# Rotating images by 180 degrees: whole 64 KB rows, three rotating slots, three transfers each way

## Chip, cores, metric

One core of a Trainium2 chip. The metric is the device time in microseconds; lower is better. The experiments ran on two chips (5, 6, 10 and 11 on one, the rest on the other), four to six executions each, always beside the kernel before, whose median was 123.67 to 123.75 us there.

## The reference

```python
def setup_inputs():
    batch, c, h, w = 32, 3, 256, 256
    return {"x": np.random.randn(batch, c, h, w).astype(np.float32)}

def reference(x):
    return np.rot90(x, k=2, axes=(-2, -1)).astype(np.float32)
```

There are 96 images of 256 KB. Rotating by 180 degrees reverses the 65,536 elements of each image. Nothing is computed: 25.17 MB come in, are reversed, and go out.

## The kernel before

Each image is cut into eight blocks of 32 KB. A pass takes 32 images: the first four blocks of each in `tinF`, the last four in `tinB`. Reversing the order of the blocks is left to the transfers' access patterns; reversing inside a block is done by VectorE, by copies of 128x4096 elements with a negative step. Each copy writes its own 16 KB tile, of which four rotate, and each tile is stored at once.

```python
# ... NG = 32 images, S = 8 blocks, BLK = 8192 elements, HB = 4096, Q = 4
tin_pool  = ctx.enter_context(tc.tile_pool(name="tin",  bufs=2))
tout_pool = ctx.enter_context(tc.tile_pool(name="tout", bufs=4))
for pp in range(n_pass):                      # 3 passes
    # ...
    nc.sync.dma_start(out=tinF[:, :], in_=x3[nsl, 0:Q, :])
    nc.sync.dma_start(out=tinB[:, :], in_=x3[nsl, S - 1:Q - 1:-1, :])

    tF0 = tout_pool.tile([P, HB], x.dtype, tag="t")
    nc.vector.tensor_copy(out=tF0[:, :], in_=tinB[:, 2 * HB - 1:HB - 1:-1])
    nc.scalar.dma_start(out=o4[nsl, 0:Q, 0, :], in_=tF0[:, :])
    # ... three more copies like this (tB0, tF1, tB1), each with its store
```

Of the kernel before, what the change touches and what calls it, by code (L numbers as in the profile page):

```python
# [2 lines left out]

os.environ.setdefault("NEURON_RT_ULTRASERVER_MODE", "4")

# [4 lines left out]


@with_exitstack
def kernel(
    ctx: ExitStack,
    tc: tile.TileContext,
    x: bass.AP,
    out: bass.AP,
):
    nc = tc.nc  # L20
    P = 128

    B, C, H, W = x.shape
    N = B * C
    L = H * W

    NG = 32
    Q = P // NG
    S = 2 * Q
    BLK = L // S  # L30

    HB = BLK // 2

    x3 = x.rearrange("b c h w -> (b c) (h w)").rearrange(
        "n (s e) -> n s e", s=S)
    o4 = out.rearrange("b c h w -> (b c) (h w)").rearrange(
        "n (s j f) -> n s j f", s=S, f=HB)

    tin_pool = ctx.enter_context(tc.tile_pool(name="tin", bufs=2))
    tout_pool = ctx.enter_context(tc.tile_pool(name="tout", bufs=4))  # L40

    n_pass = N // NG

    for pp in range(n_pass):
        nsl = slice(pp * NG, (pp + 1) * NG)
        tinF = tin_pool.tile([P, BLK], x.dtype, tag="F")
        tinB = tin_pool.tile([P, BLK], x.dtype, tag="B")
        nc.sync.dma_start(out=tinF[:, :], in_=x3[nsl, 0:Q, :])  # L48
        nc.sync.dma_start(out=tinB[:, :], in_=x3[nsl, S - 1:Q - 1:-1, :])

        tF0 = tout_pool.tile([P, HB], x.dtype, tag="t")
        nc.vector.tensor_copy(out=tF0[:, :], in_=tinB[:, 2 * HB - 1:HB - 1:-1])  # L52
        nc.scalar.dma_start(out=o4[nsl, 0:Q, 0, :], in_=tF0[:, :])

        tB0 = tout_pool.tile([P, HB], x.dtype, tag="t")
        nc.vector.tensor_copy(out=tB0[:, :], in_=tinF[:, 2 * HB - 1:HB - 1:-1])  # L56
        nc.scalar.dma_start(out=o4[nsl, S - 1:Q - 1:-1, 0, :], in_=tB0[:, :])

        tF1 = tout_pool.tile([P, HB], x.dtype, tag="t")
        nc.vector.tensor_copy(out=tF1[:, :], in_=tinB[:, HB - 1::-1])  # L60
        nc.scalar.dma_start(out=o4[nsl, 0:Q, 1, :], in_=tF1[:, :])

        tB1 = tout_pool.tile([P, HB], x.dtype, tag="t")
        nc.vector.tensor_copy(out=tB1[:, :], in_=tinF[:, HB - 1::-1])  # L64
        nc.scalar.dma_start(out=o4[nsl, S - 1:Q - 1:-1, 1, :], in_=tB1[:, :])


# [1 line left out]
_INS = ['x']  # L69
_OUTS = [((32, 3, 256, 256), 'float32')]  # L70


# [23 lines left out]
```

## Time and profile before

| | before |
|---|---|
| time, median | 123.75 us (123.7 to 123.9) |
| span of the profiled execution | 122.3 us |
| loads | 6 of 4 MB, rows of 32 KB, SyncE's queue (q1) |
| stores | 12 of 2 MB, rows of 16 KB, ScalarE's queue (q10) |
| VectorE | 12 copies, 27.2 us, 22% of the span |

Some words used below: a *packet* is what one transfer engine moves for a queue at one time, one row of a transfer here; a few bytes that only raise a semaphore are a packet too. A transfer is *issued* by an instruction of its queue's engine, and it has *landed* when its semaphore reports that all its data is there.

One view: that of who waited for whom. Its columns are total wait, number of waits, and the longest, in us.

```profile
DVE tF L52 <- DMA tinB<-in_x_dram: 41.2, 2, 23.4
DVE tF L60 <- DMA out_dram<-tF: 14.7, 2, 12.2
DVE tB L56 <- DMA out_dram<-tB: 11.1, 2, 8.4
```

VectorE stands still for up to 12 us until a store has left its tile. That costs nothing: the transfer engines have other tiles and loads in their queues all the while, and are busy for 99.6% of the time from 2.1 to 121.1 us.

### The profile page before, as it was taken

The numbers are of one execution on the slowest core, as the hardware profiler recorded it, in microseconds if no ns is written. First come the engines' busy times: TensorE is split into PE (matmuls) and PEld (weight loads), VectorE is DVE, ScalarE is ACT, GpSimd is POOL, SyncE is SP. The second block draws the span as 40 slices with busy tenths as digits, with TensorE's granted clock in tenths as the row PEclk, the third lists the DMA queues.
The fourth block names the chain that finished last, engine by engine and source line by source line (L and its number), as shares of the span: only waits on it lengthen the run. The fifth ranks groups of instructions, "written<-read, shape, count | busy, mean of one in ns | idle before, by whom it ended". The sixth has DMA issues, their size and how long they took to land.

```text
span 122.3 us, 93 instructions
## 1 busy us (share of the span) xinstructions
DVE 27.2 (22%) x12; POOL 0.2 (0%) x4
## 2 busy tenths in 40 slices
DVE  0000000399500000610160003307337156100000
POOL 0000000000000000000000000000000000000000
DMA  5798989899999998999999999999999999999992
GB/s 171 343 472 386 472 386 482 375 482 359 348 450 407 466 429 386 472 423 397 439 455 413 477 434 391 413 429 434 429 434 434 439 429 434 429 439 434 429 429 113
DMA packets 2592, 50.33 MB, mean 412 GB/s; under 512 B 288, under 2 KB 288, under 8 KB 288
## 3 DMA queue, kind: packets, MB, share of 16 engines
q1 hardware_dynamic: 864, 25.17, 48.9%
q10 hardware_dynamic: 1728, 25.17, 48.0%
HBM read 25.17 MB, written 25.17 MB: 412 GB/s over the span
## 4 chain that ended last, share of the span: by engine, by line
DMA 69%; DVE 11%; another core or an unknown queue 4%; SPq 0%; issue 0%; DVEq 0%
DMA out_dram<-tF 37%; DMA tinB<-in_x_dram 18%; DMA out_dram<-tB 14%; DVE tB L64 4%; DVE tF L60 4%; DVE tF L52 2%; DVE tB L56 2%; SPq L48 0%; DVEq L64 0%; DVEq L60 0%
## 5 line engine op out<-in xcount | busy, mean ns | idle before, releaser
L52 DVE COPY tF<-tinB 128x4096 f32<-128x4096 f32 x3 | 6.9, 2294 | 43.8 <-DMA tinB<-in_x_dram 41.2
L60 DVE COPY tF<-tinB 128x4096 f32<-128x4096 f32 x3 | 6.9, 2291 | 14.7 <-DMA out_dram<-tF 14.7
L56 DVE COPY tB<-tinF 128x4096 f32<-128x4096 f32 x3 | 6.9, 2292 | 11.1 <-DMA out_dram<-tB 11.1
L64 DVE COPY tB<-tinF 128x4096 f32<-128x4096 f32 x3 | 6.9, 2291 | 7.6 <-DMA out_dram<-tB 7.6
L80 POOL MEMSET const-bfloat16-1.0<- 128x1 bf16 x1 | 0.1, 102 | 0.0
L80 POOL MEMSET const-uint8-127<- 128x1 uint8 x1 | 0.1, 102 | 0.0
L80 POOL MEMSET const-float32-0.0<- 128x1 f32 x1 | 0.1, 99 | 0.2 <-issue 0.2
L80 POOL MEMSET const-float32-1.0<- 128x1 f32 x1 | 0.1, 99 | 0.0
## 6 DMA issues: line engine op xcount, KB each, us to landing
tinF<-in_x_dram SPq DMA_DIRECT2D x3, 4096.0 KB, 32.2
tinB<-in_x_dram SPq DMA_DIRECT2D x3, 4096.0 KB, 32.9
out_dram<-tF ACTq DMA_DIRECT2D x6, 2048.0 KB, 20.0
out_dram<-tB ACTq DMA_DIRECT2D x6, 2048.0 KB, 23.1
```

What stands on the lines that cost most here:

```text
L52: nc.vector.tensor_copy(out=tF0[:, :], in_=tinB[:, 2 * HB - 1:HB - 1:-1])
L56: nc.vector.tensor_copy(out=tB0[:, :], in_=tinF[:, 2 * HB - 1:HB - 1:-1])
L60: nc.vector.tensor_copy(out=tF1[:, :], in_=tinB[:, HB - 1::-1])
L64: nc.vector.tensor_copy(out=tB1[:, :], in_=tinF[:, HB - 1::-1])
L80: nc = _bacc.Bacc("TRN2", target_bir_lowering=False, num_devices=1)
```

## The change

The intent: fewer and larger transfers, with the longest row that stays contiguous in a partition, for the same 192 KB of each partition. An image becomes four rows of 64 KB. Three slots A, B and C of 64 KB rotate: load 0 into A, load 1 into B, turn A into C, load 2 into A, turn B into C, turn A into B. A turn is still four copies of 128x4096, but there is one store for all four. Turns 0, 1 and 2 below are these reversals; that two queues "take turns" on an engine is another matter.

```diff
-    tin_pool = ctx.enter_context(tc.tile_pool(name="tin", bufs=2))
-    tout_pool = ctx.enter_context(tc.tile_pool(name="tout", bufs=4))
+    pool = ctx.enter_context(tc.tile_pool(name="slots", bufs=1))
...  (S = 4 rows an image, E = 16384 elements, CH = 4 copies of F = 4096)
+    def load(g, slot):
+        t = pool.tile([P, E], x.dtype, tag=slot, name=f"in{g}")
+        nc.sync.dma_start(out=t[:, :], in_=x3[g * NG:(g + 1) * NG, :, :])
+        return t
+    def turn(g, t, slot):
+        r = pool.tile([P, E], x.dtype, tag=slot, name=f"out{g}")
+        for c in range(CH):
+            lo, hi = E - (c + 1) * F, E - c * F
+            src = t[:, hi - 1::-1] if lo == 0 else t[:, hi - 1:lo - 1:-1]
+            nc.vector.tensor_copy(out=r[:, c * F:(c + 1) * F], in_=src)
+        nc.scalar.dma_start(out=o3[g * NG:(g + 1) * NG, ::-1, :], in_=r[:, :])
...  (the loop over passes with its four copies and four stores goes)
+    a = load(0, "A")
+    b = load(1, "B")
+    turn(0, a, "C")
+    a = load(2, "A")
+    turn(1, b, "C")
+    turn(2, a, "B")
```

More of the change, by code (lines that the diff above doesn't have):

```diff
@@ L25 @@
     L = H * W
-    NG = 32
-    Q = P // NG
-    S = 2 * Q
-    BLK = L // S
-    HB = BLK // 2
+    S = 4
+    NG = P // S
+    E = L // S
+    CH = 4
+    F = E // CH
     x3 = x.rearrange("b c h w -> (b c) (h w)").rearrange(
         "n (s e) -> n s e", s=S)
-    o4 = out.rearrange("b c h w -> (b c) (h w)").rearrange(
-        "n (s j f) -> n s j f", s=S, f=HB)
-    tin_pool = ctx.enter_context(tc.tile_pool(name="tin", bufs=2))
-    tout_pool = ctx.enter_context(tc.tile_pool(name="tout", bufs=4))
@@ L42 @@
-    n_pass = N // NG
-    for pp in range(n_pass):
-        nsl = slice(pp * NG, (pp + 1) * NG)
-        tinF = tin_pool.tile([P, BLK], x.dtype, tag="F")
-        tinB = tin_pool.tile([P, BLK], x.dtype, tag="B")
-        nc.sync.dma_start(out=tinF[:, :], in_=x3[nsl, 0:Q, :])
-        nc.sync.dma_start(out=tinB[:, :], in_=x3[nsl, S - 1:Q - 1:-1, :])
-        tF0 = tout_pool.tile([P, HB], x.dtype, tag="t")
-        nc.vector.tensor_copy(out=tF0[:, :], in_=tinB[:, 2 * HB - 1:HB - 1:-1])
-        nc.scalar.dma_start(out=o4[nsl, 0:Q, 0, :], in_=tF0[:, :])
-        tB0 = tout_pool.tile([P, HB], x.dtype, tag="t")
-        nc.vector.tensor_copy(out=tB0[:, :], in_=tinF[:, 2 * HB - 1:HB - 1:-1])
-        nc.scalar.dma_start(out=o4[nsl, S - 1:Q - 1:-1, 0, :], in_=tB0[:, :])
-        tF1 = tout_pool.tile([P, HB], x.dtype, tag="t")
-        nc.vector.tensor_copy(out=tF1[:, :], in_=tinB[:, HB - 1::-1])
-        nc.scalar.dma_start(out=o4[nsl, 0:Q, 1, :], in_=tF1[:, :])
-        tB1 = tout_pool.tile([P, HB], x.dtype, tag="t")
-        nc.vector.tensor_copy(out=tB1[:, :], in_=tinF[:, HB - 1::-1])
-        nc.scalar.dma_start(out=o4[nsl, S - 1:Q - 1:-1, 1, :], in_=tB1[:, :])
+    o3 = out.rearrange("b c h w -> (b c) (h w)").rearrange(
+        "n (s e) -> n s e", s=S)
```

## The prediction

> **What bounds the kernel now.** I read four views: the slices and queues of the page, the queue tables of two stretches, and the engine in order of time. First the page, which says that nothing but the transfer engines can be the bound.
>
> ```profile
> span 122.3 us, 93 instructions
> ...
> DVE 27.2 (22%) x12; POOL 0.2 (0%) x4
> ...
> DMA  5798989899999998999999999999999999999992
> ...
> q1 hardware_dynamic: 864, 25.17, 48.9%
> q10 hardware_dynamic: 1728, 25.17, 48.0%
> ```
>
> VectorE works 22% of the span. The DMA row is full in every slice but the first few and the last. The queue of the loads (q1) and that of the stores (q10) fill 48.9 + 48.0 = 96.9% of 16 engines' span; asked for the stretch from 2.1 to 121.1 us, the same table gives 50.2 + 49.4 = 99.6%. So there is no hole in the middle, VectorE's waits on the stores cost nothing, and what lies outside is a start of 2.1 us and an end of 1.2 us.
>
> Second, how fast the engines work when only one direction runs (stores alone, 80 to 105 us), and third how the two directions share (30 to 45 us).
>
> ```profile
> DMA packets 738, 10.78 MB, mean 431 GB/s; under 512 B 80, under 2 KB 80, under 8 KB 80
> ...
> q10 hardware_dynamic: 738, 10.78, 100.7%
> ```
>
> ```profile
> q1 hardware_dynamic: 142, 4.13, 67.3%
> q10 hardware_dynamic: 135, 2.03, 31.6%
> ```
>
> In the first, 738 - 80 = 658 data packets of 16 KB take 100.7% of 16 x 25 us: 0.612 us each. From 5 to 20 us, loads alone, 203 packets of 32 KB fill 102.7% of 16 x 15 us: 1.214 us each. The durations of single packets in the trace are steadier still, 0.611 and 1.213. Twice 0.611 is 1.222, so a packet carries some 10 ns of its own and the rest is bytes. In the second fence the packets of both queues are nearly equal in number, 142 to 135, and the bytes go 2 to 1 with the packet sizes: an engine takes turns, one packet each. That is the fact on which the change depends.
>
> Fourth, when a store gets going behind a backlog of loads. The engine view in order of time:
>
> ```profile
> 23.36 2.29 DVE L52 COPY tF<-tinB 128x4096 f32<-128x4096 f32 x1 [23.36 <-DMA tinB<-in_x_dram]
> 25.56 2.29 DVE L56 COPY tB<-tinF 128x4096 f32<-128x4096 f32 x1
> 25.68 0.62 ACTq L53 DMA_DIRECT2D out_dram<-tF  x1
> 27.77 2.29 DVE L60 COPY tF<-tinB 128x4096 f32<-128x4096 f32 x1
> 27.88 0.55 ACTq L57 DMA_DIRECT2D out_dram<-tB  x1
> 29.97 2.29 DVE L64 COPY tB<-tinF 128x4096 f32<-128x4096 f32 x1
> 30.08 0.55 ACTq L61 DMA_DIRECT2D out_dram<-tF  x1
> 32.28 0.54 SPq L48 DMA_DIRECT2D tinF<-in_x_dram  x1
> ```
>
> The first store is issued at 25.68, but the queue table of 25.7 to 29.8 us holds packets of q1 alone; the first of q10 starts at 29.8, and the last engine gets to it at about 31.8. An issue on idle engines takes 1.4 us (first load issued at 0.73, first packet at 2.13); here it is 4.1 to 6.1 us: two or three load packets of 1.21 us that stand ahead are done first. Meanwhile four copies take 3 x 2.20 + 2.29 = 8.9 us.
>
> **What the Trainium skill says.** "DMA: Bandwidth & Descriptors", section "Queues, rings and completion order": each DMA engine goes round its queues at packet granularity. The 142 to 135 packets agree. The same section says that the semaphore's increment comes after the data of that engine; the 288 packets under 512 B (18 DMAs on 16 engines) are these, and in the trace such a packet also takes a turn in its queue. Section "Where 436 GB/s comes from" of that page gives a ceiling of 435.2 GB/s; the trace has 431 in the store-only stretch, so no change of shape can win much. "VectorE: DVE Perf Modes", "The perf-mode tier table", gives an fp32 SBUF copy of 2048 elements 1227 ns; the trace has 2294 ns for 4096, less than double, and the changed kernel keeps that same 128x4096 reversed copy.
>
> **The change, part by part.** Bytes are the same, 25.17 MB each way, and so are the twelve copies. SBUF stays at 192 KB a partition. 18 transfers become 6 of 8.39 MB; the packets should grow to 64 KB if a row goes as one packet. The copies no longer write four rotating 16 KB tiles, each stored as soon as it is turned, but one 64 KB slot that is stored when all four are done; and the second and third turns have no slot of their own: turn 1 writes C, which store 0 must leave first; turn 2 writes B, which turn 1 must have read.
>
> Gain. A 64 KB packet would be 4 x 0.602 + 0.010 = 2.417 us (0.602 is the difference of the two packet times above). Per engine 48 packets: 116.0 us. Before: 48 x 1.213 + 96 x 0.611 = 116.9 us, and 18 small ones. So 0.9 to 1.0 us is saved.
>
> Loss, followed in time on one engine. (1) Load 0 lands at 23.3 as the first 8.39 MB do now. Copies to 32.2; store 0 and load 2 are issued at 32.25 (now, too, the last of the first group's four stores goes at 32.29). (2) Load packet k ends at about 3.1 + 2.417 k (the slow first packets cost 0.6 in the trace). The store's first packet comes 4.1 to 6.1 us after issue, at 36.4 to 38.4, rounded up to the end of a 64 KB packet: packet 14 ends at 36.9, packet 15 at 39.35. I take 15. (3) Store 0 and the loads then take turns one to one: 8 store packets and 7 loads, 15 x 2.417 = 36.3, plus 0.7 for the stretched packets seen where the first store mixes in: the eighth ends at 76.3. By then 15 + 7 = 22 of 24 load packets are done; all loads are through at 76.3 + 2 x 2.417 = 81.1. (4) The semaphore packet waits for one more load packet, and the landing follows some 0.5 us after it, as for the first store now: 76.3 + 2.4 + 0.5 = 79.2. (5) Only now may turn 1 start in C: 8.9 us, store 1 is issued at 88.1, first packet 1.4 later at 89.5. From 81.1 to 89.5 the transfer engines have nothing: 8.4 us. (6) Turn 2 runs from 88.1 to 97 behind store 1, hidden; store 2 queues up behind it. 16 packets x 2.417 = 38.7, plus 1.0 for staggered and slow starts, plus the end of 1.2: span 89.5 + 40.9 = 130.4. The timed figure is 1.45 above the profile's span now (123.75 to 122.3): 131.9 us.
>
> With 14 load packets ahead the store ends one packet (2.4 us) earlier and three loads are left: 129.5. With 16 (three whole packets ahead of the store, as some engines had), 134.3. I put the middle at 131: the 15 case, leaning to 14 as 4.1 us alone would give it.
>
> **The rivals.** *Hidden anyway.* The loads that are left cover the 8.9 us of copies, and only the larger packets count: 123.75 - 1.0 = 122.8. For it speaks that VectorE waits up to 12 us for stores now at no cost. Against it: those waits are hidden by a backlog of other loads or of three other stored tiles, and here at most 2 or 3 load packets (5 to 7 us) are left against a semaphore, four copies and an issue, some 13 us. For the hole to close, store 0 would have to finish with six load packets left. *Short delay.* The store gets in 1.4 us after issue, behind the running packet only: 13 loads ahead, four left, hole near 3.6 us, time near 127.1. The 4.1 us of the trace speak against it, though that store was followed by three more issues, which may have held it up. *Rows cut smaller.* If rows go as 32 KB packets, the turns stay one to one: the store begins near 37, its 16 packets and 15 loads take 37.6 + 0.7, landing near 77.3, store 1 starts near 87.7, and the time is near 130: the same mechanism. Were loads cut and stores not, stores would get two thirds and the hole would vanish, 123; nothing speaks for that. *VectorE as the bound:* its total stays at 27 us, and no engine is near full. It matters only at the one place where its four copies stand alone.
>
> **Range and chances.** Predicted 131.0, 8 in 10 between 127.0 and 134.5: the low end is the short delay, the high end 16 packets ahead. Two per cent faster is 121.3, only 0.5 above 116.0 of packets, 2.1 of start, 1.2 of end and 1.45 outside the profile, with no slow packet and no hole at all, so 0.02. Within 2% needs the hole under 3.5 us: 0.08. Slower: 0.90.
>
> **What would show it.** In the changed profile: one hole in the DMA row, some 6 to 9 us, a little after two thirds of the span, with VectorE busy in it; the first copy of the second turn waiting for the first store, the longest wait after the start; six issues of 8192 KB; 64 KB packets, 384 a queue with 48 small ones each; store 0's landing 44 to 49 us after its issue; in the mixed stretch equal bytes on both queues. A full DMA row with about 122 us would prove the step from packets to turns wrong; a hole of another size, the count of load packets ahead of store 0; a stretch of lower GB/s, that large packets run at the same rate.

## More of the kernel before

Every execution was at a granted clock of 1.000, so only like is compared with like. The timed figure is some 1.8 us above the span of the same execution, which runs from its first to its last instruction.

## The result

The changed kernel takes 127.34 us (median of 4: 126.83, 126.83, 127.84, 128.04) against 123.8 us for the kernel before on the same chip. The ratio is 1.0293, 95% interval 1.0250 to 1.0337. Ratios here are the mean time of one kernel's fast runs over that of the other's of the same rounds, so not quite the ratio of the medians. The result is right on all outputs.

The page of the changed kernel (span, the DMA row of the 40 slices, the two queues):

```profile
span 125.0 us, 65 instructions
...
DMA  9779879977909779779977977709877977977790
...
q1 hardware_dynamic: 432, 25.17, 47.9%
q10 hardware_dynamic: 432, 25.17, 46.5%
```

Two things are to be seen. The queues hold 432 packets each, 384 of data and 48 small ones: a row of 64 KB is one packet. And their shares fell, from 96.9% to 94.4% of a longer span. The zeros in the DMA row need care: a slice is 3.1 us, a packet now 2.4 us, and the 16 engines run nearly in step, so a slice in which few packets start looks empty (the early zero near 35 us is such a one). Asking for single stretches settles it. The columns are the stretch and its length, VectorE's busy time, GpSimd's, the clock, the share of the transfer engines and GB/s:

```profile
2.10:81.00 78.90, 15.11 (x7) 0.00 (x0) 1.00 0.97 414
81.30:84.90 3.60, 3.57 (x3) 0.00 (x0) 1.00 0.00 0
84.90:124.00 39.10, 7.73 (x4) 0.00 (x0) 1.00 0.99 429
```

From 81.3 to 84.9 us no data moves at all, and VectorE is busy in 3.57 of the 3.60 us. From its last load packet to its first packet of store 1, an engine is idle for 3.9 us on the mean. Before and after it, the engines are as full as before the change. The chain of waits (start, duration, what) and VectorE's waits say what the hole is made of:

```profile
31.53 43.14 DMA out_dram<-out
74.66 0.03 issue
74.69 0.05 DVEq L56
74.74 0.05 issue
74.79 8.91 DVE out L56 x4
```

```profile
DVE out L56 <- DMA out_dram<-out: 43.3, 1, 43.3
```

Store 0 is issued at 31.53 and lands at 74.66. Only then may turn 1 write slot C. Its four copies take 8.91 us, to 83.70; store 1 is issued at 83.73, and its first packet starts at 84.95. The loads had their last packet through between 80.9 and 81.5. The wait that was 12 us long and free before is 43 us long, and the last 3.9 us of what follows it find the queues empty.

### The profile page after: what moved, and what is told of

It reads as the page before. It is cut to its first block, busy times and chain, and to the rows that moved or that the text cites. A ratio compares the mean times of both kernels' runs of the same rounds, so it can differ in the third digit from the quotient of the medians.

```text
span 125.0 us, 65 instructions
## 1 busy us (share of the span) xinstructions
DVE 26.7 (21%) x12; POOL 0.2 (0%) x4
## 3 DMA queue, kind: packets, MB, share of 16 engines
q1 hardware_dynamic: 432, 25.17, 47.9%
q10 hardware_dynamic: 432, 25.17, 46.5%
## 4 chain that ended last, share of the span: by engine, by line
DMA 52%; DVE 20%; DVEq 2%; issue 0%
DMA out_dram<-out 34%; DVE out L56 20%; DMA in<-in_x_dram 17%; DVEq L90 2%; DVEq L56 0%
## 5 line engine op out<-in xcount | busy, mean ns | idle before, releaser
L56 DVE COPY out<-in 128x4096 f32<-128x4096 f32 x12 | 26.7, 2289 | 65.9 <-DMA out_dram<-out 43.3
```

The lines of the kernel that those rows point to most:

```text
L56: nc.vector.tensor_copy(out=r[:, c * F:(c + 1) * F], in_=src)
```

## The experiments

All edits are against the changed kernel unless said otherwise. The theory under test, called "turns" below: the two queues take turns packet by packet; how many load packets are left when store 0 lands decides how much of the chain behind it (landing, four copies, issue) is covered. The rivals: packets of 64 KB cost time as such; the scheme of slots costs as such; VectorE, at 21% of the span, cannot matter.

### 1 and 2: is the bare chain on the path?

First, each copy of the second turn twice.

```diff
-            nc.vector.tensor_copy(out=r[:, c * F:(c + 1) * F], in_=src)
+            for _ in range(2 if g == 1 else 1):
+                nc.vector.tensor_copy(out=r[:, c * F:(c + 1) * F], in_=src)
```

> The changed kernel with each of the four copies of the second turn done twice. Theory: these copies lie on the path that ends the hole, so the hole grows from 3.8 to 12.7 us: 135.7 us, 8.9 more than the changed kernel's 126.8. Rival 'copies are hidden beside transfers' (VectorE is busy 21% of the span): no change, 127.

Measured: 136.06 us (135.55 to 136.78), ratio to the kernel before 1.0996. The profiled execution has a span of 133.8 us, 8.8 more than the changed kernel's, and in the view of single stretches the hole has grown to 81.3 to 93.7 us:

```profile
81.30:93.70 12.40, 12.37 (x7) 0.00 (x0) 1.00 0.00 0
```

Four copies more, 8.8 us more: these copies lie on the path in full.

Second, the same for the third turn (`g == 2`).

> The changed kernel with each of the four copies of the third turn done twice. Theory: they lie beside store 1, which runs to 104.4 us; the doubled turn ends near 101.4 and store 2 is issued before store 1 ends: no change, 126.8 to 128. A rival in which VectorE work as such costs time gives 135.7 here as for the second turn.

Measured: 127.32 us (126.58 to 127.87), ratio 1.0282, as the changed kernel. The same 8.8 us of VectorE work, put beside store 1, is free. So it is neither VectorE's load as such nor "copies are hidden": where they stand decides.

### 3 and 4: packet sizes, with a side effect

To shift the turns, one direction's rows are cut in two. First the loads:

```diff
-        nc.sync.dma_start(out=t[:, :], in_=x3[g * NG:(g + 1) * NG, :, :])
+        for h in (slice(0, E // 2), slice(E // 2, E)):
+            nc.sync.dma_start(out=t[:, h], in_=x3[g * NG:(g + 1) * NG, :, h])
```

> The changed kernel with each load as two transfers of 32 KB rows, stores and copies untouched (the half that the first copy needs is loaded last, so nothing starts earlier). Theory (turns): with 32 KB load packets against 64 KB store packets store 0 gets two thirds of the bandwidth, its eight packets end near 63 us instead of 71.4 to 73.9, it lands near 65, turn 1 is done near 74, and store 1 starts while loads are still queued: no hole (before the copies' end the DMA row is full), 123.0 us, a little faster than the kernel before. Rival 'large packets cost': loads at 32 KB give back at most half of the loss, 125 us or more, and the hole stays. Rival 'the slot scheme itself costs' (two turns that must wait for a slot): about 127, as the changed kernel.

Measured: 130.05 us (129.9 to 130.08), ratio 1.0507: a plain miss by 7 us. The trace shows the old hole gone (the queues move 421 GB/s from 60 to 80 us) and a new one from 101 to 107.4. The view of single stretches first, then the engines in order of time (start, duration, what, and in brackets the wait before it):

```profile
101.00:107.40 6.40, 4.49 (x2) 0.00 (x0) 1.00 0.07 31
```

```profile
77.08 4.49 DVE L57 COPY out<-in 128x4096 f32<-128x4096 f32 x2 [0.95 <-DMA in<-in_x_dram]
101.68 4.49 DVE L57 COPY out<-in 128x4096 f32<-128x4096 f32 x2 [20.10 <-DMA in<-in_x_dram]
```

The third turn's last two copies waited 20 us for one half of load 2, which landed at 101.7. On 14 of the 16 engines the loads' data was through by 84.1 us. Two had fallen behind between 45 and 67 us, where some of their 32 KB packets took up to 2.1 us instead of 1.21; store 1 then came between their last loads, turn by turn, to 98.9. So a late load packet is caught by the store's turns just as a late store is by the load's. Why two engines fell behind is open; all four runs have the time. The promise that nothing would start early was not kept either: the first two copies ran at 12.83 us, on the half that had landed. The built program has the copies of that half in front: the order of the source is not kept where the data allow another.

Then the stores:

```diff
-        nc.scalar.dma_start(out=o3[g * NG:(g + 1) * NG, ::-1, :], in_=r[:, :])
+        for h in (slice(E // 2, E), slice(0, E // 2)):
+            nc.scalar.dma_start(out=o3[g * NG:(g + 1) * NG, ::-1, h], in_=r[:, h])
```

> The changed kernel with each store as two transfers of 32 KB rows, both issued after all four copies; loads at 64 KB. Theory (turns): store 0 now gets one third while loads are queued, the ten load packets that are left are through near 75 us, store 0 ends last near 81, and the whole chain of landing, four copies and issue (0.8 + 8.9 + 1.3 = 11 us) lies bare: hole near 11 us, 134 us, 7 us slower than the changed kernel. Rival 'large packets cost': smaller store packets help, below 127.

Measured: 129.77 us (129.54 to 130.03), ratio 1.0484: slower, so the rival falls, but 4 us short of what was expected. Store 0 did land at 81.8, as expected. But the hole is 6.2 us, not 11: one half is issued after two copies, not four (at 27.19 in the first turn); the built program again has another order than the source. The two copies that are missing from the chain are 4.4 us.

### 5 and 6: packet sizes alone

Both experiments again, with one transfer each, so that nothing can start early. The two halves of a row are swapped in the slot, which makes two 32 KB packets of it; the copies take that into account.

```diff
-        nc.sync.dma_start(out=t[:, :], in_=x3[g * NG:(g + 1) * NG, :, :])
+        nc.sync.dma_start(out=t[:, :].rearrange("p (h e) -> p h e", h=2)[:, ::-1, :],
+                          in_=x3[g * NG:(g + 1) * NG, :, :].rearrange("n s (h e) -> n s h e", h=2))
...
-            lo, hi = E - (c + 1) * F, E - c * F
+            j = (CH - 1 - c + CH // 2) % CH
+            lo, hi = j * F, (j + 1) * F
```

> As the first experiment, but each load stays one transfer and only its packets shrink to 32 KB (the two halves of a row land swapped in the slot, and the copies read them so). Nothing can start early: store 0 is issued near 31.5 us. Theory (turns): store 0 gets two thirds, lands near 65, no hole at the old place near 81. What decides the time is whether the last load lands before turn 2 is wanted: if it keeps off store 1's turns it lands by 87 us and the time is 123.0; if two transfer engines run slow as in the first experiment it lands near 100 and a second hole of about 7 us puts it at 130. Rival 'the early first half made the trouble in the first experiment': then 123 here. Rival 'large packets cost': 125 to 127 with the old hole.

Measured: 123.56 us (123.49 to 123.72), ratio to the kernel before 0.9990 (0.9974 to 1.0005). The queue tables (packets, MB, share of the engines) of the changed kernel from 51.5 to 70.8 us, and of this one from 38 to 60 us:

```profile
q1 hardware_dynamic: 64, 4.19, 50.2%
q10 hardware_dynamic: 64, 4.19, 50.1%
```

```profile
q10 hardware_dynamic: 102, 6.68, 70.1%
q1 hardware_dynamic: 96, 2.62, 27.6%
```

With equal packets the bytes are shared evenly; with load packets half as long the store gets 70%. Store 0 lands at 66.7 instead of 74.66, turn 1 is over at 75.7, and loads are still moving until 84 us (on one engine until 87): there is no hole. Only the packets of the loads are smaller; bytes, slots and number of copies are the same, and the whole loss is gone.

The stores alone (the reversal of the rows moves to the load, because the store's pattern would need too many dimensions):

```diff
-        nc.scalar.dma_start(out=o3[g * NG:(g + 1) * NG, ::-1, :], in_=r[:, :])
+        nc.scalar.dma_start(out=o3[g * NG:(g + 1) * NG, :, :].rearrange("n s (h e) -> n s h e", h=2),
+                            in_=r[:, :].rearrange("p (h e) -> p h e", h=2)[:, ::-1, :])
...  (load with ::-1 over the rows; copy c writes block (c + 2) % 4)
```

> As the second experiment, but each store stays one transfer after all four copies and only its packets shrink to 32 KB (halves swapped in the slot; the order of the four rows is turned in the load instead of the store). Theory (turns): store 0 is issued at 31.5 us, gets one third, ends last near 81, and landing, four copies and issue lie bare: hole near 11 us, 134 us, 4.3 more than the second experiment, in which the first half went out after two copies. Rival: below 130.

Measured: 134.53 us (134.09 to 135.05), ratio 1.0876. The queue table from 40 to 70 us gives the store a good third; the view of single stretches shows the whole chain as a hole:

```profile
q1 hardware_dynamic: 143, 8.32, 64.0%
q10 hardware_dynamic: 144, 4.72, 36.4%
```

```profile
82.60:92.90 10.30, 9.99 (x5) 0.00 (x0) 1.00 0.00 0
```

Same bytes, same slots, same copies, smaller store packets: 7 us slower. Smaller load packets: 3.8 us faster. A price on large packets as such would have made both faster; the turns explain both signs, and experiment 9 has packets of 64 KB both ways without a loss.

### 7 and 8: the two terms of the hole

The hole can be shrunk from two sides: by sending store 0 off earlier, or by shortening the chain behind it. One edit serves both: ScalarE takes 6144 of the 16384 elements of a row and VectorE 10240 in one instruction.

```diff
+        if g == 0:      # experiment 7; g == 1 in experiment 8, all turns in experiment 9
+            n = 5 * E // 8
+            nc.vector.tensor_copy(out=r[:, 0:n], in_=t[:, E - 1:E - n - 1:-1])
+            nc.scalar.copy(out=r[:, n:E], in_=t[:, E - n - 1::-1])
+        else:           # the four copies as they were
```

> The same sharing, for the first turn only: store 0 is issued near 28.2 instead of 31.5 us, so one load packet fewer is ahead of it and one more is left behind it. Theory: store 0 lands 2.4 us earlier, the hole falls from 3.8 to 1.4 us, 124.4 us (125.5 in the slower of the two groups in which the changed kernel's times fall). If the count of packets ahead does not follow the issue: no change, 126.8.

Measured: 124.50 us (124.31 to 125.47), ratio 1.0075. Store 0 is issued at 28.17, behind 13 load packets an engine instead of 14: its first packets start at 34.9 to 35.6 instead of 37.4 to 37.9. It lands one packet earlier, so that turn 1 begins at 72.30 instead of 74.79 (engines in order of time), and store 1 starts at 82.45 instead of 84.95. That is 2.5 us in the trace, one packet of 2.42 us.

```profile
72.30 8.90 DVE L61 COPY out<-in 128x4096 f32<-128x4096 f32 x4 [44.22 <-DMA out_dram<-out]
```

> The same sharing, for the second turn only: the load and store turns stay as they are, and the chain in the hole is 3.3 us shorter. Theory: hole from 3.8 to 0.5 us, 123.5 us (124.6 in the slower group). Rival 'VectorE does not bind': no change.

Measured: 125.14 us (124.33 to 125.30), ratio 1.0098. The gain over the changed kernel (126.89 us, experiment 12) is 1.7 us, where 3.3 was expected. The engines in order of time show why:

```profile
75.35 1.28 ACT L56 ACT_TABLE_LOAD   x1 [75.35 <-DMA out_dram<-out]
75.41 5.50 DVE L55 COPY out<-in 128x10240 f32<-128x10240 f32 x1 [43.74 <-DMA out_dram<-out]
76.65 5.31 ACT L56 COPY out<-in 128x6144 f32<-128x6144 f32 x1
```

ScalarE loads its table first, inside the chain. The Trainium skill, page "ScalarE: Activation LUTs", section "What ACT_TABLE_LOAD costs", gives the load some 1283 ns; here it is 1.28 us. In experiments 7 and 9 it falls at 0.7 us, where ScalarE has nothing to do. So the copies took 6.6 us instead of 5.6. The rest is that in this execution they began at 75.35, 0.6 us later than in the changed kernel's profile; why is open. Store 1 starts at 83.2 to 83.35, and the hole is some 2 us.

### 9: both together, all packets at 64 KB

> The changed kernel, all packets at 64 KB, with every turn shared: VectorE turns 10240 of the 16384 elements of a row in one instruction, ScalarE the other 6144. A turn should take some 5.6 us in place of 8.9 (VectorE's copies run at 2290 ns for 4096 elements, so 5.5 for its part; ScalarE's speed is not measured yet). Theory: store 0 goes out 3.3 us earlier and the chain in the hole is 3.3 us shorter, together more than the hole of 3.8 us: hole closed, 122.8 to 123.1 us. Rival (packets of 64 KB cost as such, or the slot wait does): 125 or more.

Measured: 123.77 us (123.54 to 124.15), ratio 1.0004 (0.9985 to 1.0024). There is no hole: store 1 is issued at 77.87 while loads are queued. The view of single stretches (VectorE, ScalarE and GpSimd busy, then as before):

```profile
70.00:85.00 15.00, 8.52 (x2) 8.44 (x2) 0.00 (x0) 1.00 0.97 419
```

With the same slots and the same packets as in the changed kernel, but no hole, the whole loss is gone: neither the slots nor packets of 64 KB cost time as such. But the 0.7 to 1.0 us that large packets should have brought over the kernel before are not there. This term of the prediction fails, and it is taken up below.

### 10: slot C in two halves

The loads stay at 64 KB. Slot C becomes two tiles of 32 KB; each half is stored after its two copies, and each copy of the second turn waits for its own half only.

```diff
-        r = pool.tile([P, E], x.dtype, tag=slot, name=f"out{g}")
+        for h in range(2):
+            r = pool.tile([P, E // 2], x.dtype, tag=f"C{h}", name=f"out{g}_{h}")
...          (two copies into r, then its store; turn 2 writes the halves of B likewise)
```

> The changed kernel with slot C as two tiles of 32 KB a partition: each is stored as soon as its two copies are done, and a copy of the second turn waits for the store of its own half only. Loads stay at 64 KB. Theory: the first half's store lands near 60 us, its copies are done and stored again before the second half's store ends near 81, so there is always a store in the queue and no hole: 122.8 to 123.0 us, about 0.7% faster than the kernel before and 3.5% faster than the changed one. Rival 'large packets or the wait for a slot cost': 125 or more. Risk: the queue order of the last load as in the first experiment.

Measured: 123.19 us (123.11 to 123.71), ratio 0.9969 (0.9950 to 0.9988). It beats both kernels, the one before by 0.3%, where 0.7% was expected. In the trace turn 1's first half is copied from 62.77 to 67.27 and stored while the second half's store still runs, to 82.42. From 40 to 120 us the engines move 433 GB/s without a break.

```profile
62.77 4.50 DVE L64 COPY out<-in 128x4096 f32<-128x4096 f32 x2 [31.20 <-DMA out_dram<-out]
```

```profile
40.00:80.00 40.00, 4.50 (x2) 0.00 (x0) 1.00 1.00 433
```

### 11: larger packets without the slots

The kernel before, with two output tiles of 32 KB for its four of 16 KB, so that only the store packets grow.

```diff
-    tout_pool = ctx.enter_context(tc.tile_pool(name="tout", bufs=4))
+    tout_pool = ctx.enter_context(tc.tile_pool(name="tout", bufs=2))
...  (two copies into the two halves of a [P, BLK] tile, then one store of it)
```

> The kernel before with its four rotating 16 KB output tiles made two of 32 KB, each stored after two copies: store packets of 32 KB, everything else as before. Per engine 48 x 1.213 in place of 96 x 0.611 us, 0.44 less, and six semaphore packets fewer: theory 123.2 to 123.3 us if no hole opens (a landing, two copies and an issue, 0.8 + 4.5 + 1.3 = 6.6 us, are covered by the other tile's store of 9.7 us). Rival 'packet size is worth nothing': 123.75. If two tiles are too few: above 124.

Measured: 124.28 us (124.11 to 124.54), ratio 1.0051 (1.0035 to 1.0067): 0.6 us slower, where 0.4 to 0.5 us faster was expected. The trace has no hole, and its span of 122.4 us is near that of the kernel before's profile, 122.3, which was a slower execution of that kernel (the timed ones beside this experiment had 121.7 to 122.1). Where the 0.6 us lies is open.

### 12: the changed kernel again

> The changed kernel itself, for comparison on this chip, and because its times fall in two groups, 126.8 and 127.9 to 128.0. Theory: both groups have the hole. If the profile catches the slower group, the hole is longer there by about 1 us or the start is later by as much; if it catches the faster, nothing is learned of it.

Measured: 126.89 us (126.73 to 127.60), ratio 1.0268. The hole is in the same place, with zero bytes from 81.3 to 84.9 us. The profile caught the faster group of times again. What makes the slower group, about 1 us longer here and in experiments 1 and 2, is open.

## Why the prediction was right, and where its sizes were off

**The figure.** 131.0 was predicted, 7.25 us slower; 127.34 was measured, 3.5 us slower. That is inside the range of 127.0 to 134.5, but only just, and two of the four executions (126.83) lie under it. That the range held is in good part luck: its low end was set by the "short delay", whose mechanism did not happen. Two of the signs failed: the hole was to be 6 to 9 us and store 0 to land 44 to 49 us after its issue (43.1 measured). The prediction said what a hole of another size would mean, a wrong count of load packets ahead of store 0; that is half of it.

**The bound and the turns: right.** The transfer engines bind; a row is a packet; the queues take turns one to one. Experiments 5 and 6 turn this into a control: 70% or 36% of the bandwidth for store 0, and 123.56 or 134.53 us.

**Step 5, the hole: right in place and kind, too large.** A hole of 8.4 us from 81.1 on was predicted; 3.9 us from 81.2 on were measured. The end of the loads was right to 0.1 us, and so were the copies (8.9). The term that was mis-sized is the landing of store 0: 79.2 predicted, 74.66 measured. Two steps account for it.

**Step 2, the load packets ahead of store 0.** I took 15. The trace has 14: store packets start at 37.4 to 37.9 us, 5.9 to 6.4 after the issue. Load 0 landed, and store 0 was issued, 0.7 us earlier than assumed (31.53 against 32.25), and the rounding up to the next packet was wrong; one packet is 2.4 us. The prediction names this as its choice and gives the time with 14 as 129.5.

**Step 3, seven loads between eight stores.** It was six. Load 1 ends in the middle, and its semaphore packet takes the load queue's turn. The queue table of 49 to 51 us shows it:

```profile
DMA packets 32, 1.05 MB, mean 524 GB/s; under 512 B 16, under 2 KB 16, under 8 KB 16
...
q10 hardware_dynamic: 16, 1.05, 121.1%
q1 hardware_dynamic: 16, 0.00, 0.5%
```

All 16 engines give the load's turn to a packet of 4 bytes, and the store goes on at once with its next row. That is another 2.4 us. The prediction had noted that semaphore packets take turns, but applied it to the store's alone (step 4, where it holds: 71.2 to 71.9 for the eighth packet's end, one load packet, then the landing). 129.5 less 2.4 is 127.1; measured were 126.8 in the faster group. Followed through, the 5.1 us between the 131.9 of the working and 126.8 are 4.5 of an earlier landing, 0.8 of a shorter end (40.1 us from store 1's first packet to the end of the span, 40.9 predicted), less 0.4 outside the span (1.83 us, 1.45 predicted); rounding leaves 0.2. Experiment 7 moves step 2 by one packet and finds it in the time; experiments 1 and 8 move the chain of step 5.

**The gain from large packets: too large, and not seen in the time.** 0.9 to 1.0 us was predicted. The packet itself was right: 2.42 us, 2.417 worked out. From the page, the packets' time per engine is (48.9 + 48.0)% of 122.3 = 118.5 us before and (47.9 + 46.5)% of 125.0 = 118.0 us after, and in experiment 9 (49.4 + 47.7)% of 121.8 = 118.3 us. Added packet by packet, without the rounding of the shares, it is 118.5, 118.1 and 118.2: 0.3 to 0.4 us. Part of what is lost is in the mixing. The queue table of the load packets that start from 33.7 to 34.5 us, just before the first store:

```profile
q1 hardware_dynamic: 16, 1.05, 452.9%
```

Sixteen packets in 452.9% of 0.8 us are 3.6 us each, against 2.42 otherwise. Summed over all packets that start from 25 to 45 us, the excess over the undisturbed time is 1.2 us per engine (0.9 before; 1.4 in experiment 9, 1.7 in experiment 10). The prediction carried 0.7 for it, from small packets. Where the remaining 0.3 to 0.4 us go is open, the more so as the profiled execution of the kernel before was one of the slowest (122.3 us of span, where the timed ones had 121.7 to 122.3); that also made the 1.45 us outside the span, used in the prediction, some 0.3 to 0.4 too small. Experiments 9 and 11 together say that packets above 16 or 32 KB bring nothing here that shows in the time.

**Step 6, turn 2 hidden: right,** as experiment 2 shows. **The rivals:** "hidden anyway" and "VectorE as the bound" fall by experiments 1 and 2. "Short delay" predicted 127.1 with a hole of 3.6 us, near the measured figures, but not by its mechanism: the store came after 14 loads, not 13, and some 5.9 us after its issue. "Rows cut smaller" did not happen, since a row went as one packet; its aside that with the loads alone cut the hole would vanish, at 123, is experiment 5, with 123.56.

## What to carry to other kernels

When two queues fed the same transfer engines here, the packet sizes set the shares (70% to 28% at 64 against 32 KB): give the longer packets to the stream that someone waits for, and count what is left in the other queue when the wait ends, against landing, compute and issue behind it. A buffer that must be stored before it can be written again is free only while something else is queued; splitting it in two, each half stored as soon as it is full, kept a transfer in the queue for no more memory (experiment 10). Count the semaphore packets in the turns, and build "one part alone" experiments so that nothing else can start earlier, since half a transfer lets half the work move.

## What the Trainium skill lacked or had wrong

- "DMA: Bandwidth & Descriptors", "Queues, rings and completion order", has engines drain a packet of typically 9 to 17 descriptors per turn. Here a turn is one row: 142 to 135 packets of 32 and 16 KB in the kernel before, 64 to 64 of 64 KB after. The page does not draw the consequence that row lengths set the shares (70% to 28% at 64 against 32 KB), nor that a semaphore packet takes a turn (16 engines, 49 to 51 us).
- No page says how long a transfer waits behind a queue that is already full: 4.1 to 6.1 us from issue to first packet at 32 KB load packets, 5.9 to 6.4 at 64 KB (31.53 to 37.4 and 37.9).
- The same page, "Latency and other measured facts", has about 0.6 us to the first byte. It does not say from when. On idle engines the traces show 1.4 us from the start of the issue (0.73 to 2.13, before), 1.0 (0.73 to 1.73, after) and 1.2 (83.73 to 84.95); the issue itself takes 0.60, 0.37 and 0.56 us of these, and counted from its end they are 0.80, 0.63 and 0.66, near the page's figure.
- No page has the stretching of packets just before a second direction joins: 3.6 us instead of 2.42 for one 64 KB load packet on each engine. Its cause was not tested.
- "Perfetto Trace Analysis", "DMA Optimizations", says that larger transfers saturate bandwidth better, with examples up to 8 KB; that section has nothing beyond. With rows of 16 KB in 2 MB transfers the stores alone ran at 431 GB/s; with 64 KB in 8 MB, 429.
